# A two-layer DiT block on one core: attention scores laid out with keys on the partitions, row maxima from a separate pass, sums of exponentials on GpSimd

## Chip, cores and metric

One core of a Trainium2 chip. The metric is the device time of one execution in microseconds (us); three runs of the kernel before give a median of 3380.52 us.

## What is computed

Two layers on 2048 tokens of 1024 features and 256 context tokens. The even layer modulates its input, multiplies it by `w_in`, and cuts the product into queries, keys, values and gates of two kinds of heads. It runs softmax attention over context and tokens, multiplies the heads' outputs by silu of the gates, and projects them by `w_out`. The odd layer is a gated MLP with a mixing of tokens in chunks; the change leaves it alone.

```python
def block_attention(q, k, v, scale):          # for blocks of queries
    sc = jnp.einsum('bqhgd,bthd->bhgqt', qi, k).astype(jnp.float32) * scale
    p = jax.nn.softmax(sc, axis=-1).astype(v.dtype)
    return jnp.einsum('bhgqt,bthe->bqhge', p, v)

def even_heads(h, ...):
    cq, ckv, kr, g_a, qb, kb, vb, g_b = jnp.split(h, idx, axis=-1)
    q_a = (rms_norm(cq, a_q_norm) @ a_w_uq).reshape(bsz, n, A_HEADS, A_NOPE + A_ROPE)
    kv_a = (rms_norm(ckv, a_kv_norm) @ a_w_ukv).reshape(bsz, n, A_HEADS, A_NOPE + A_V)
    q_b = rms_norm(qb.reshape(bsz, n, B_HEADS, B_HD), b_q_norm)
    k_b = rms_norm(kb.reshape(bsz, n, B_KV_HEADS, B_HD), b_k_norm)
...
```

There are eight heads of kind A (a latent of low rank; 64 plain and 32 rotary dimensions, values of 64) and eight of kind B (64 dimensions, four query heads to each of two key heads). All rotary parts get an axial rotation. A `rms_norm` divides by the root mean square over features: over 384 latent features for A's queries, over the 64 of a head for B's.

## The kernel before, in words

All products run in a one-pass 32-bit float format (`F32R`) that keeps about 12 significant bits. To keep precision, an operand is split into a high part `h` and a low part `l` (`split`, L57 to L63): ScalarE copies the value into `h`, VectorE subtracts it from the value to give `l`; with `pool=True` GpSimd does both (L59, L60). A product of two split operands is high by high, high by low and low by high.

**Phase 1** computes the product with `w_in` in two halves of the tokens, each in chunks of 512 (`CH`). Activations are feature-major: features on the partitions, tokens along the row. A product (`gemm`) is 24 matmuls of 512 columns into one of the PSUM buffers `ps`; what follows from it is put in `queue` and issued behind the next product (`flush`). B's queries (the loop over `j` in `range(4)`, two chunks each, so eight products per half) are squared on ScalarE, copied with the gain, rotated by `rope` (shuffle L212, products with the tables on GpSimd L213 and VectorE L214, sum L215), split and stored to `QB` by `put`. Their square sums go by `join` and a selection matrix `sel` into one PSUM tile `ssq`; A's query latents (`C3`) are split unnormalised and multiplied by `uq`, and `query_norms` makes one factor 1/rms per query and head from all these sums (`e.rq`). Keys are normalised at once: `rnorm` (L240 to L247) gets the sum on every row from a matmul with ones, takes the root on ScalarE and the RECIPROCAL on VectorE (L246). Between the products run the gates' products and, at a rate per weight tile, the sums for modulation rows needed later (`later_rows`, L267, L276).

**Attention** runs over 16 heads by four groups of 512 queries: 64 groups, the heads of A first, each over 18 tiles of 128 keys (2304 keys). For each of the four tiles of 128 queries of a group, `score` makes the scores with queries on the partitions, in three thirds of 768 keys: three products (A) or two (B, where the 64 dimensions of both parts are stacked on 128 partitions), each as 512 and 256 columns (L605). VectorE scales a third by `e.rq` into SBUF and takes its running maximum (L608); L611 joins the three maxima. `expo` takes exponentials on ScalarE in place (L617), with the sum of each third in `e.parts`. `turn` brings them to keys on partitions: four fp32 transposes of 128x128 on TensorE per key tile (L624), a split of the transposed 128x512 (L62 on ScalarE, L63 on VectorE; every ninth tile on GpSimd by a copy `pf`). `mul` adds V by `ph` and V by `pl` to the output in PSUM (L643), V's high and low parts side by side in 128 columns. At a group's last tile the two halves are added (L647, L648), multiplied by the gate on GpSimd (L649) and stored. `recip` makes 1/sums from `e.parts` in the last four groups, and phase 3 multiplies by them.

The order of the work in attention is written out by hand: each call is a unit with a place in the stream of key tiles, and `units` is sorted by it (L666 and behind). Scores run a group and six tiles ahead, `mul` runs `LAG` = 3 tiles behind `turn`, and the first five tiles of a group some more (`LATE`), since the output's PSUM bank must come free.

**Phase 3** (the output projection and the odd layer) follows; `ring` lays out its first activations in the buffers of keys, values and queries while the last heads run.

Tile pools give each tag a ring of `bufs` buffers; a new tile waits until its buffer's last reader is done.

## Time and profile before

| | us |
|---|---|
| median of three runs (3379.19 to 3383.6) | 3380.52 |
| span of the profiled execution | 3370.8 |
| TensorE busy (17594 instructions) | 3275.9 |
| VectorE busy (4070) | 2472.9 |
| ScalarE busy (3648) | 2000.3 |
| GpSimd busy (603) | 730.2 |

The profile gives for the profiled execution its span, from the first to the last instruction, and no time apart from it; the times of the runs come from outside the program and lie some 10 us higher. Busy times overlap between engines. A matmul's listed duration contains its pipeline, so two that follow each other overlap in the timeline: the distance of their starts, the step, is what the stream costs. The granted clock is the one that the throttle gave TensorE, as a share of full speed.

### The profile page before, as it was taken

What the parts mean: (1) busy time and instruction counts of PE and PEld (TensorE: products, weight loads), DVE (VectorE), ACT (ScalarE), POOL (GpSimd) and SP (SyncE); (2) the same over time, 40 slices, a digit from 0 to 9 for tenths busy, and PEclk for the clock granted to TensorE, in tenths of its full rate; (3) what the DMA queues carried; (4) which work ended last, traced back from release to release, by engine and by line L of the source; (5) the groups of instructions that cost most, each with busy time, mean ns of one, the idle gap of its engine ahead of it and who ended that gap; (6) DMA issues with size and microseconds to landing.
All of it is one profiled execution on the core that took longest, in us unless ns stands there. A gap on an engine that the chain in (4) does not pass through costs nothing.

```text
span 3370.8 us, 47622 instructions
## 1 busy us (share of the span) xinstructions
PE 3275.9 (97%) x17594; PEld 2754.0 (82%) x17594; DVE 2472.9 (73%) x4070; ACT 2000.3 (59%) x3648; POOL 730.2 (22%) x603
## 2 busy tenths in 40 slices
PE   7999999999999999999999999999999899999998
PEld 3787667888888888888888888888778788788787
DVE  4647663488888888888989999999665665765846
ACT  3333332377777777778888888887444253353342
POOL 3413332111111111111222122223222302301201
PEclk9999999999999999999999999999999999999999
DMA  6466654612211221122100010002633343433332
GB/s 230 129 202 207 192 178 142 199 30 55 55 45 39 59 59 42 38 66 61 27 20 23 23 41 23 20 23 49 203 95 113 108 142 113 128 122 113 105 95 75
DMA packets 149083, 311.01 MB, mean 92 GB/s; under 512 B 17762, under 2 KB 43682, under 8 KB 145522
## 3 DMA queue, kind: packets, MB, share of 16 engines
q1 hardware_dynamic: 141058, 280.56, 27.7%
q0 software_dynamic: 7712, 27.28, 2.6%
q8 instruction: 138, 2.26, 0.3%
q14 instruction: 95, 0.78, 0.1%
q10 hardware_dynamic: 80, 0.13, 0.0%
HBM read 237.45 MB, written 70.47 MB: 91 GB/s over the span
## 4 chain that ended last, share of the span: by engine, by line
PE 81%; DVE 6%; issue 4%; DMA 3%; ACT 2%; POOL 1%; SPq 0%; POOLq 0%; ACTq 0%; DVEq 0%
PE s L605 20%; PE o L643 16%; PE pt L624 15%; PE acc L866 3%; PE acc L867 3%; PE acc L868 3%; PE acc L769 3%; PE acc L770 3%; PE acc L771 3%; PE ps L176 3%; PE ps L177 3%; PE ps L178 3%; DMA w<-in_o_w_in 1%; DMA wr<-in_o_w_mod 1%; DMA xr<-in_xT 1%
## 5 line engine op out<-in xcount | busy, mean ns | idle before, releaser
L608 DVE TENSOR_SCALAR_CACHE_REDUCE pr<-s,rq 128x768 f32<-128x768 f32 x768 | 776.0, 1011 | 144.7 <-PE s L605 123.6
L605 PE MATMUL s<-k,q 96*128 96x512 f32 (+3 forms) x3840 | 801.5, 339 | 0.1
L63 DVE TENSOR_TENSOR pl<-pt,ph 128x512 fp32r<-128x512 f32 x1032 | 700.8, 687 | 129.7 <-ACT ph L62 109.1
L62 ACT ACTIVATE ph<-pt 128x512 fp32r<-128x512 f32 x1032 | 605.4, 594 | 267.3 <-PE pt L624 256.6
L617 ACT ACTIVATE pr<-pr,mx 128x768 f32<-128x768 f32 x768 | 715.5, 932 | 58.0 <-DVE mx L611 57.7
L605 PEld LDWEIGHTS s<-k,q 96*128 96x128 f32 (+1 forms) x3840 | 635.5, 188 | 110.3 <-DVE pr L608 1.5
L624 PE MATMUL pt<-ident,pr 128*128 128x128 f32 x4608 | 682.0, 272 | 5.0 <-DVE pl L63 4.8
L624 PEld LDWEIGHTS pt<-ident,pr 128*128 128x128 f32 x4608 | 554.3, 140 | 84.7 <-DVE pl L63 5.8
L643 PE MATMUL o<-ph,v 128*128 128x512 f32 x1152 | 539.3, 468 | 0.3 <-DVE ob L648 0.3
L643 PE MATMUL o<-pl,v 128*128 128x512 f32 x1152 | 453.3, 393 | 0.0
L62 ACT ACTIVATE wh<-w 128x1024 fp32r<-128x1024 f32 x154 | 163.2, 1059 | 466.7 <-PE acc L771 221.4
L63 DVE TENSOR_TENSOR wl<-w,wh 128x1024 fp32r<-128x1024 f32 x154 | 203.5, 1321 | 252.7 <-ACT wh L62 252.6
L59 POOL TENSOR_SCALAR ph<-pf 128x512 fp32r<-128x512 f32 x120 | 74.1, 618 | 1123.0 <-ACT pf L629 1039.8
L176 PE MATMUL ps<-xh,wh 128*128 128x512 f32 (+1 forms) x640 | 249.6, 390 | 6.8 <-POOL xh L167 3.4
L177 PE MATMUL ps<-xl,wh 128*128 128x512 f32 (+1 forms) x640 | 250.2, 391 | 5.3 <-DVE xl L168 5.3
L178 PE MATMUL ps<-xh,wl 128*128 128x512 f32 (+1 forms) x640 | 249.0, 389 | 1.0 <-DVE wl L148 1.0
L643 PEld LDWEIGHTS o<-pl,v 128*128 128x128 f32 x1152 | 221.0, 192 | 5.9 <-DVE pl L63 0.2
L643 PEld LDWEIGHTS o<-ph,v 128*128 128x128 f32 x1152 | 218.7, 190 | 6.3 <-DVE ob L648 0.6
L769 PE MATMUL acc<-wh,k 128*128 128x512 f32 x384 | 155.8, 406 | 28.9 <-DVE y L903 22.6
L60 POOL TENSOR_TENSOR pl<-pf,ph 128x512 fp32r<-128x512 f32 x120 | 154.8, 1290 | 10.0
L770 PE MATMUL acc<-wl,k 128*128 128x512 f32 x384 | 154.4, 402 | 0.5 <-DVE wl L63 0.5
L771 PE MATMUL acc<-wh,k 128*128 128x512 f32 x384 | 153.1, 399 | 0.0
(283 smaller groups left out, 4897.0 us busy)
## 6 DMA issues: line engine op xcount, KB each, us to landing
w<-in_wug SPq DMA_DIRECT2D x64, 512.0 KB, 3.5
wr<-in_w SPq DMA_DIRECT2D x38, 512.0 KB, 4.5
w<-in_e_w_out SPq DMA_DIRECT2D x32, 512.0 KB, 3.5
w<-in_o_w_in SPq DMA_DIRECT2D x32, 512.0 KB, 4.2
w<-in_o_w_out SPq DMA_DIRECT2D x32, 512.0 KB, 3.5
wr<-in_e_w_mod SPq DMA_DIRECT2D x24, 512.0 KB, 6.3
wr<-in_o_w_mod SPq DMA_DIRECT2D x24, 512.0 KB, 4.0
VA<-va SPq DMA_DIRECT2D x18, 512.0 KB, 4.6
```

Of the source, the lines that this page charges most:

```text
L62: e.nc.scalar.activation(h, src, AF.Copy)
L63: e.nc.vector.tensor_tensor(out=l, in0=src, in1=h.bitcast(F32), op=ALU.subtract)
L176: nc.tensor.matmul(out, lhsT=wh(k), rhs=xh(k), start=i == 0, stop=False)
L177: nc.tensor.matmul(out, lhsT=wh(k), rhs=xl(k), start=False, stop=False)
L178: nc.tensor.matmul(out, lhsT=wl(k), rhs=xh(k), start=False, stop=i == n - 1)
L605: nc.tensor.matmul(ps[:, n0:n0 + w], lhsT=a, rhs=b[:, c * SC + n0:c * SC + n0 + w], start=u == 0, stop=u == len(prods) - 1)
L608: nc.vector.tensor_scalar(out=prs[n][:, c * SC:(c + 1) * SC], in0=ps[:, :SC], scalar1=e.rq[:, 4 * g + j, r:r + 1], scalar2=None, op0=ALU.m ...
L617: nc.scalar.activation(x, x, AF.Exp, bias=stats[n][:, 3:4], accum_out=e.parts[:, 4 * g + j, h, c:c + 1])
L624: nc.tensor.transpose(pt[:, j * P:(j + 1) * P], prs[4 * i + j][:, t * P:(t + 1) * P], e.ident)
L643: nc.tensor.matmul(acc[i], lhsT=kv[h][1][:, t, :], rhs=p, start=t + u == 0, stop=t + u == NTT)
L769: nc.tensor.matmul(ps[t], lhsT=h[:, ts], rhs=w[0][:, k, :], start=first, stop=False)
L770: nc.tensor.matmul(ps[t], lhsT=h[:, ts], rhs=w[1][:, k, :], start=False, stop=False)
```

## The change

In phase 1, B's queries are normalised at once like the keys: for each product, `rnorm` (now L241 for its RECIPROCAL, with the softmax scale folded into the root) and a multiply (L346) before `put`. A's latents are normalised before their split (`finish` behind L443, four times three tiles), so `sel`, `ssq`, `join`, `query_norms` and `e.rq` go.

In attention, `score` puts keys on the partitions: one tile of 128 keys by 512 queries, three (A) or two (B) products (L646). The negative maximum of each query is an extra row of the queries against a row of ones in the keys, so that the scores leave PSUM already reduced by it. Exponentials are taken twice from PSUM: into `ph`, rounded to the high part (L655), and in place (L656); VectorE subtracts for `pl` (L657). On tile 8 (A) or tiles 4, 9 and 14 (B), GpSimd splits a copy. `peak` computes the maxima one group ahead, from high parts alone, with queries on the partitions: eight times two matmuls of 512 into a PSUM tile `m` of two banks with one buffer and a reduction of 1024 columns (L611, L613), then four matmuls of 256 and one reduction (L617, L619), and L621 joins them; `row` transposes the four columns of maxima (L629) and ScalarE writes them into the queries' extra row (L631). The sums of exponentials are added tile by tile on GpSimd from `ph` (L663), 14 adds per group of A, 10 of B, 5 in the last four groups; the remaining tiles and the total are summed on TensorE by the matrix `last` (L680, L682), and the low parts by a column of ones behind V. `mul` adds V by `ph` into `oh` (L677) and V's high part by `pl` into `ol` (L678). Queries are loaded two groups ahead.

```diff
+                    def finish(c=c, j=j, o=halves(sq), t=t):
+                        r = rnorm(o, bones, CH, HD, SB)
+                        nc.vector.tensor_tensor(out=t, in0=t, in1=r, op=ALU.mult)
+                        put(t, e.QB[:, j * P:(j + 1) * P, c * CH:(c + 1) * CH])
...
+                        def finish(c=c, o=halves(sqs[c])):
+                            r = rnorm(o, ones, CH, QR, SA)
+                            for i in range(3):
+                                t = ts[c, i]
+                                nc.vector.tensor_tensor(out=t, in0=t, in1=r, op=ALU.mult)
+                                C3[c, i] = unit()
+                                split(e, *C3[c, i], t)
...
+        def peak(i, m):
...
+            pm = pp.tile([P, 2 * CH], F32, name="m", tag="m", bufs=1)
+            if m < 8:
+                j, half = divmod(m, 2)
+                for u in range(2):
+                    k0 = half * 2 * CH + u * CH
+                    nc.tensor.matmul(pm[:, u * CH:(u + 1) * CH], lhsT=Q[:r, 0, j * P:(j + 1) * P], rhs=K[:r, 0, k0:k0 + CH],
+                                     start=True, stop=True)
+                nc.vector.tensor_reduce(out=stats[i][:, j, half:half + 1], in_=pm, axis=AX.X, op=ALU.max)
...
+            ps = pp.tile([P, CH], F32, name="s", tag="s", bufs=4)
...
+                prods = [(K[:m + 1, 0, ks], Q[:m + 1, 0, :]), (K[:m, 1, ks], Q[:m, 0, :]), (K[:m, 0, ks], Q[:m, 1, :])]
...
+                prods = [(K[:, 0, ks], Q[:, 0, :]), (K[:HD + 1, 1, ks], Q[:HD + 1, 1, :])]
...
+            ph = sp.tile([P, CH], F32R, name="ph", tag="ph", bufs=LAG + 4)
+            pl = sp.tile([P, CH], F32R, name="pl", tag="pl", bufs=LAG + 4)
...
+                nc.scalar.activation(ph, ps, AF.Exp)
+                nc.scalar.activation(ps, ps, AF.Exp)
+                nc.vector.tensor_tensor(out=pl, in0=ps, in1=ph.bitcast(F32), op=ALU.subtract)
...
+                nc.gpsimd.tensor_tensor(out=a, in0=tot[i].bitcast(F32), in1=ph.bitcast(F32), op=ALU.add)
...
+            nc.tensor.matmul(oh, lhsT=V[:, t, :2 * DV], rhs=ph, start=first, stop=end)
+            nc.tensor.matmul(ol[:DV + 1], lhsT=V[:, t, DV:2 * DV + 1], rhs=pl, start=first, stop=False)
+            if t not in shares(i)[1]:
+                nc.tensor.matmul(ol[:DV + 1], lhsT=last[:, :DV + 1], rhs=ph, start=False, stop=False)
+            if end:
+                nc.tensor.matmul(ol[:DV + 1], lhsT=last[:, :DV + 1].bitcast(F32), rhs=tot.pop(i), start=False, stop=True)
...
+            for m in range(9):
+                units.append((p0 + 1.6 * m, 1, peak, i, m))
+            units.append((p0 + 1.6 * 8 + 1.9, 1, row, i))
```

TensorE in an A group, mid-stream, before (`pt` is the transposed tile, `pr` the exponentials, `o` the output):

```order
L624 MATMUL pt<-ident,pr 128x128 x4
L643 MATMUL o<-ph,v 128x512
L643 MATMUL o<-pl,v 128x512
L605 MATMUL s<-k,q 128x512
L605 MATMUL s<-k,q 128x256
L605 MATMUL s<-k,q 128x512
L605 MATMUL s<-k,q 128x256
L605 MATMUL s<-k,q 128x512
L605 MATMUL s<-k,q 128x256
L624 MATMUL pt<-ident,pr 128x128 x4
```

and in the change, at the end of the maxima's pass (`m` the scores for the maxima, `nm` the negative maxima):

```order
L611 MATMUL m<-k,q 128x512 x2
L646 MATMUL s<-q,k 128x512 x3
L677 MATMUL oh<-ph,v 128x512
L678 MATMUL ol<-pl,v 65x512
L646 MATMUL s<-q,k 128x512 x3
L677 MATMUL oh<-ph,v 128x512
L678 MATMUL ol<-pl,v 65x512
L617 MATMUL m<-k,q 128x256 x4
```

The transposes are gone, scores are 512 columns wide, and the maxima's matmuls stand between the key tiles.

VectorE around the end of a group, before (`L648` is the add of the output's halves):

```order
L648 TENSOR_TENSOR ob<-o,ob 64x512
L608 TENSOR_SCALAR pr,mx<-s,rq 128x768
L63 TENSOR_TENSOR pl<-pt,ph 128x512 x2
L608 TENSOR_SCALAR pr,mx<-s,rq 128x768
L63 TENSOR_TENSOR pl<-pt,ph 128x512
```

and in the change:

```order
L613 TENSOR_REDUCE mx<-m 128x1
L657 TENSOR_TENSOR pl<-s,ph 128x512
L689 TENSOR_TENSOR ob<-oh,ob 64x512
L691 TENSOR_TENSOR ob<-ol,ob 64x512
L657 TENSOR_TENSOR pl<-s,ph 128x512
L613 TENSOR_REDUCE mx<-m 128x1
```

The scalings of 768 have gone, reductions of 1024 have come, and the output takes two adds.

VectorE in phase 1, B's queries of the second half, before (`L267` is a modulation row's sum):

```order
L212 STREAM_SHUFFLE sq<-t 128x512
L214 TENSOR_TENSOR sq<-sq,ts 128x512
L267 SCALAR_TENSOR_TENSOR acc<-wr,sc,acc 128x512
L215 TENSOR_TENSOR t<-t,sq 128x512
L267 SCALAR_TENSOR_TENSOR acc<-wr,sc,acc 128x512
L63 TENSOR_TENSOR oo<-t,oo 128x512
L148 TENSOR_TENSOR wl<-wr,wh 128x1024
```

and in the change (the lines of the rotation are now L211 to L214, of the sum L262, of the split L65):

```order
L241 RECIPROCAL sq<-sq 128x512
L211 STREAM_SHUFFLE sq<-t 128x512
L346 TENSOR_TENSOR t<-t,sq 128x512
L213 TENSOR_TENSOR sq<-sq,ts 128x512
L262 SCALAR_TENSOR_TENSOR acc<-wr,sc,acc 128x512
L65 TENSOR_TENSOR oo<-t,oo 128x512
L214 TENSOR_TENSOR t<-t,sq 128x512
```

Each product of B's queries gets a RECIPROCAL and a multiply, in front of its split.

## Rows read from the trace of the kernel before

**Rows 1.** The page: busy time by engine; the chain by engine; one of its pieces.

```profile
PE 3275.9 (97%) x17594; PEld 2754.0 (82%) x17594; DVE 2472.9 (73%) x4070; ACT 2000.3 (59%) x3648; POOL 730.2 (22%) x603
...
PE 81%; DVE 6%; issue 4%; DMA 3%; ACT 2%; POOL 1%; SPq 0%; POOLq 0%; ACTq 0%; DVEq 0%
...
88.50 3.35 DVE sq L246
```

**Rows 2.** Windows: stretch, length, busy time by engine, granted clock, DMA share, GB/s.

```profile
92.00:150.00 58.00, 56.79 (x260) 45.01 (x259) 41.74 (x53) 20.23 (x38) 31.23 (x21) 1.00 0.52 151
396.00:465.00 69.00, 59.29 (x247) 44.98 (x248) 65.07 (x79) 19.83 (x36) 34.32 (x22) 0.98 0.70 215
1000.00:1200.00 200.00, 200.00 (x1253) 177.20 (x1251) 162.33 (x312) 151.66 (x300) 35.68 (x35) 1.00 0.16 45
1800.00:1900.00 100.00, 100.00 (x635) 88.30 (x633) 90.79 (x183) 86.78 (x174) 20.40 (x20) 1.00 0.09 23
```

**Rows 3.** Timeline of PE in a group of A: start, duration, instruction.

```profile
1010.13 0.60 PE L624 MATMUL pt<-ident,pr 128*128 128x128 f32 x4
1010.48 0.48 PE L643 MATMUL o<-ph,v 128*128 128x512 f32 x1
1010.80 0.39 PE L643 MATMUL o<-pl,v 128*128 128x512 f32 x1
1011.03 1.21 PE L605 MATMUL s<-k,q 96*128 96x512 f32 x6
1012.07 0.60 PE L624 MATMUL pt<-ident,pr 128*128 128x128 f32 x4
```

**Rows 4.** Timeline of DVE: last add of two groups of A, then of B.

```profile
769.43 0.67 DVE L648 TENSOR_TENSOR ob<-o,ob 64x512 f32<-64x512 f32 x1
...
798.21 0.67 DVE L648 TENSOR_TENSOR ob<-o,ob 64x512 f32<-64x512 f32 x1
...
1598.31 0.68 DVE L648 TENSOR_TENSOR ob<-o,ob 64x512 f32<-64x512 f32 x1
...
1622.96 0.67 DVE L648 TENSOR_TENSOR ob<-o,ob 64x512 f32<-64x512 f32 x1
```

**Rows 5.** Attention's first score (chain) and phase 3's first matmul (timeline).

```profile
660.08 1.06 PE s L605 x6
...
2383.22 0.63 PE L769 MATMUL acc<-wh,k 128*128 128x512 f32 x2
```

**Rows 6.** Timeline of PE in phase 3: first and last of 55 matmuls.

```profile
2500.16 0.39 PE L866 MATMUL acc<-v,wh 128*128 128x512 f32 x1
...
2512.40 0.39 PE L866 MATMUL acc<-q,wh 128*128 128x512 f32 x1
```

**Rows 7.** Timeline of PE in phase 1: fp32 matmuls of 512 columns.

```profile
502.66 2.74 PE L276 MATMUL rows<-acc,pick 128*2 128x512 f32 x6
```

**Rows 8.** Timeline of DVE in a group of A, then in phase 1.

```profile
1019.28 1.01 DVE L608 TENSOR_SCALAR_CACHE_REDUCE pr<-s,rq 128x768 f32<-128x768 f32 x1
1020.21 0.68 DVE L63 TENSOR_TENSOR pl<-pt,ph 128x512 fp32r<-128x512 f32 x1
...
396.72 1.21 DVE L148 TENSOR_TENSOR wl<-wr,wh 128x1024 fp32r<-128x1024 f32 x1
397.86 0.68 DVE L63 TENSOR_TENSOR vt<-pt,vt 128x512 fp32r<-128x512 f32 x1
```

**Rows 9.** Timeline of ACT in attention: three copies from PSUM in a row.

```profile
2363.14 1.56 ACT L62 ACTIVATE ph<-pt 128x512 fp32r<-128x512 f32 x3
```

**Rows 10.** POOL's instructions on two tiles: least, median, most ns; then a group's mean.

```profile
L60 POOL TENSOR_TENSOR pl<-pf,ph x120: 1278/1288/1300, 692.7 to 2284.7; 128x512 fp32r<-128x512 f32 x120
...
L877 POOL TENSOR_TENSOR u<-u,y 128x512 f32<-128x512 f32 x32 | 63.4, 1981 | 404.3 <-ACT y L876 404.3
```

**Rows 11.** DVE in phase 1: reciprocals of the norms; one tile's sums, least, median, most ns.

```profile
L246 DVE RECIPROCAL sq<-sq 128x512 f32<-128x512 f32 x8 | 26.8, 3348 | 5.1 <-ACT sq L245 5.1
...
L215 DVE TENSOR_TENSOR t<-t,sq x32: 662/692/1580, 84.0 to 622.1; 128x512 f32<-128x512 f32 x28, 32x512 f32<-32x512 f32 x4
```

More of the change, by code (lines that the diff above doesn't have):

```diff
@@ L232, in halves, with rnorm @@
             return o
-        def join(out, lhs, o, first=True, last=True):
+        def rnorm(o, lhs, n, width, S=1.0):
+            ss = pp.tile([P, CH], F32, name="ss", tag="misc", bufs=3)
             for i in range(2):
-                nc.tensor.matmul(out, lhsT=lhs, rhs=o[:, i, :], start=first and i == 0, stop=last and i == 1,
-                                 skip_group_check=True)
-        def rnorm(o, lhs, n, width):
-            ss = pp.tile([P, CH], F32, name="ss", tag="misc", bufs=2)
-            join(ss[:, :n], lhs, o)
+                nc.tensor.matmul(ss[:, :n], lhsT=lhs, rhs=o[:, i, :], start=i == 0, stop=i == 1)
             r = tmp(P, n, "sq", 4)
-            nc.scalar.activation(r, ss[:, :n], AF.Sqrt, scale=1.0 / width, bias=e.eps)
+            nc.scalar.activation(r, ss[:, :n], AF.Sqrt, scale=1.0 / (width * S * S), bias=e.epsq[S])
             nc.vector.reciprocal(r, r)
@@ L485, in phase1 @@
                 if half == 1 and i == 1:
-                    e.first = keys(e, 0), queries(e, 0, 0)
+                    e.first = keys(e, 0), [queries(e, 0, g) for g in range(2)]
             assert not aside
@@ new lines, in attention, with shares @@
+        kv, qs, stats, pts = {}, {}, {}, {}
+        acc, tot, gates = {}, {}, {}
+        kv[0], (qs[0], qs[1]) = e.first
+        last = cp.tile([P, DV + 2], F32R, name="last")
+        nc.vector.memset(last[:, :DV].bitcast(F32), 0.0)
+        nc.vector.memset(last[:, DV:].bitcast(F32), 1.0)
+        def shares(i):
+            if i >= NW - NG:
+                return (), (0, 2, 5, 8, 11, 14)
+            if i < NH * NG:
+                return (8,), tuple(t for t in range(16) if t != 8)
+            return (4, 9, 14), tuple(t for t in range(16) if t not in (4, 7, 9, 12, 14))
@@ new lines, in row, with score @@
+        def row(i):
+            h, g = work[i]
+            nm = stats.pop(i)[1]
+            pm = pp.tile([P, 2 * CH], F32, name="m", tag="m", bufs=1)
+            for j in range(4):
+                nc.tensor.transpose(pm[:1, j * P:(j + 1) * P], nm[:, j:j + 1], e.ident)
+            dst = qs[i][NOPE + ROPE:NOPE + ROPE + 1, 0, :] if h < NH else qs[i][HD:HD + 1, 1, :]
+            nc.scalar.activation(dst, pm[:1, :CH], AF.Copy)
+        def score(s):
+            i, t = divmod(s, NTT)
+            h, g = work[i]
+            K, Q = kv[h][0], qs[i]
+            ks = slice(t * P, (t + 1) * P)
+            ps = pp.tile([P, CH], F32, name="s", tag="s", bufs=4)
+            m = NOPE + ROPE
@@ L619, in turn @@
-        def turn(s):
-            i, t = divmod(s, NTT)
-            pt = pp.tile([P, CH], F32, name="pt", tag="pt", bufs=3)
-            for j in range(4):
-                nc.tensor.transpose(pt[:, j * P:(j + 1) * P], prs[4 * i + j][:, t * P:(t + 1) * P], e.ident)
-            ph = sp.tile([P, CH], F32R, name="ph", tag="ph", bufs=LAG + 2)
-            pl = sp.tile([P, CH], F32R, name="pl", tag="pl", bufs=LAG + 2)
-            if t % 9 == 8 and i < len(work) - NG:
+                nc.tensor.matmul(ps, lhsT=a, rhs=b, start=u == 0, stop=u == len(prods) - 1)
@@ L652, in recip @@
-        def recip(b):
-            qs = slice(4 * b, 4 * b + 4)
-            nc.vector.tensor_reduce(out=e.sums[:, qs, :], in_=e.parts[:, qs], axis=AX.X, op=ALU.add)
-            nc.vector.reciprocal(e.sums[:, qs, :], e.sums[:, qs, :])
-            rp = pp.tile([P, CH], F32, name="rp", tag="pt", bufs=3)
-            for j in range(4):
-                nc.tensor.transpose(rp[:2 * NH, j * P:(j + 1) * P], e.sums[:, 4 * b + j, :], e.ident)
-            rs = sp.tile([2 * NH, CH], F32, name="rs", tag="pf", bufs=2)
-            nc.scalar.activation(rs, rp[:2 * NH, :], AF.Copy)
-            cs = slice(b * CH, (b + 1) * CH)
-            nc.sync.dma_start(e.R1[:, cs], rs)
@@ L666, in attention @@
[L666 to L674 removed]
+                acc[i] = [pp.tile([P, CH], F32, name="o" + q, tag="o" + q, bufs=1) for q in "hl"]
@@ L675, in attention @@
+        for s in range(NW * NTT):
+            units.append((s, 2, score, s))
             t = s % NTT
```

238 lines of the change are left out of this document (106 added, 132 removed).

## The prediction, made before the change was timed

> **What bounds the kernel now.** I read the page's busy times and chain first [rows 1]: TensorE (PE) is busy 97% of the 3370.8 us span and makes 81% of the chain. Then the windows [rows 2]: in both kinds of attention heads PE has no gap, at a granted clock of 1.00, while VectorE (DVE) stands at 81% (A) and 91% (B), ScalarE (ACT) at 76% and 87%, GpSimd (POOL) at 18% and 20%. So attention costs what PE streams, and a faster PE would soon meet DVE. Phase 1 is mixed: in 92 to 150 PE has 56.8 of 58 us, but in 396 to 465 only 59.3 of 69, with DVE at 65.1: there DVE paces. The chain's row at 88.50 [rows 1] is a RECIPROCAL of 3.35 us: a norm on DVE can already be exposed.
>
> The PE timeline of an A group [rows 3] gives the steps, start to start: four transposes 0.35 (1010.13 to 1010.48), the two products with V 0.32 and 0.23, a score pair of 512 and 256 columns 0.347 (1.04 for three pairs, 1011.03 to 1012.07). The first product behind the transposes costs some 0.09 more than the second; I call that a switch. A group has 36 pairs and 18 of the rest: 12.5+16.2 = 28.7. From one group's last add to the next's [rows 4] it is 28.78 in A and 24.66 in B, so the steps explain the period. Attention lasts from the first score, 660.08, to phase 3's first matmul, 2383.22 [rows 5]: 1723 us.
>
> **PE in attention.** Dense matmuls of 512 columns step by 0.227 (2500.16 to 2512.40 is 54 steps) [rows 6]. A group of A now has 54 score products, 16 maxima, 36 products with V and three sums by `last`: 109 x 0.227 = 24.7. The four maxima of 256 columns cost 0.347-0.227 each, 0.48 together. The four transposes of the maxima I put at 0.58 (0.35, two switches, rounded up). The final sum in plain fp32 runs as two instructions, like the modulation rows' sums, of 2.74/6 = 0.46 each [rows 7], 0.91, and two switches, 1.1. Together 26.9 against 28.78. B: 36+16+36+7 = 95 matmuls, 21.6, and the same 2.2: 23.7 against 24.66. So PE saves only 1.9 and 0.9 us a group: the transposes were cheap, and the maxima take most of it back.
>
> **What covers the rest of attention.** DVE: a scaling of 768 steps 0.93 (1019.28 to 1020.21), an op of 1024 steps 1.14 (396.72 to 397.86) [rows 8]. A reduction of 1024 from PSUM is not in the trace. Its bounds: 1.14, and the scaling's duration 1.01 x 1024/768 = 1.35. I take 1.15, since the row of the same width is the nearest. A subtraction of 512 steps 0.61 (0.68 less the overlap of 0.07 that the 1024 row shows). A: 9 x 1.15 + 17 x 0.61 + two adds 1.2 + 0.15 = 22.1 of 27; B, with 15 subtractions, 20.9 of 24. All reductions lie in 13 of a group's 18 key tiles; there DVE has 18.2 of PE's 20.7 us in A, 17.6 of 18.4 in B: covered, but tight in B. ACT: three ops of 512 take 1.56 [rows 9], so A's 35 exponentials 18.2, and with copies under 20.5. A tile holds one of the four `s` buffers some 4.3 us (scores 0.68, two exponentials 1.1, subtraction 0.68, a reduction in its way 1.15, hand-overs 0.7); four tiles of PE last 5.3 to 6.
>
> POOL: A has 14 adds x 1.29 (the 128x512 subtraction there, 1278 to 1300 ns) [rows 10] + 1.9 for the parts + 1.3 for the gate = 21.3; B 10 x 1.29 + 5.7 + 1.3 = 19.9. The other row of such an add, L877 in phase 3, has a mean of 1.98: the upper bound. I take 1.29, being from attention. PE's final sum waits for the last add, tile 15's, which has five tiles or 7 us. The gate product stands behind adds, and SP's store of O waits for it; what is queued behind on SP, the queries two groups ahead, has a whole group to spare. That, and the sums' way through DRAM before phase 3, I cost at nothing; without the cover attention would get the DMA share that the chain has as a whole, 3% [rows 1], 0.03 x 1723 = 52 us.
>
> With small stalls I take 27.0 and 24.0. The prologue is new: nine maxima run before the first score, and with one `m` buffer PE and DVE alternate, 9 x (0.45+1.15+0.25) and the row: 17 to 18. Nothing fills PE meanwhile; should it run slower after the gaps, some 5 more: I take 23. Attention: 23 + 32 x 27.0 + 28 x 24.0 + the last four groups with 12 sums on PE, 3 x 25 + 21 (the last has no next maxima) + 4 to drain = 1659, **-64**.
>
> **Phase 1.** The query norms move here. DVE gets 20 RECIPROCALs of 3.35 [rows 11] (16 for the QB products, four before uq), 67 us, and 28 multiplies at 0.69 (L215 on the same operands, up to 1.58 beside POOL), 19: 86 us in all. PE shows of it what DVE cannot fit. Half 0: 41.7 + 8 x 4.04 = 74.0 in 58 us, 16.0 too much; the ring of four `sq` tiles, three of them per product, lets PE lead by about two products of 24 x 0.227, 10.9: 5 exposed. Half 1: 65.1+32.3-69 = 28.4, less 10.9: 17.5. Before uq, reciprocal, multiply and split (3.35+0.69+0.68, and 1.4 for each further part) follow the square sums, with one gate product of 5.4 as cover: 5 per half, 10. The joins and small transposes that go give back 3. **+30** (bounds: +5, if idle DVE time takes all but part of the uq waits; +86, nothing hidden). POOL gets memsets of ones, SP one more query group to load, both early: nothing.
>
> Phase 3 differs by the shape of two rings and keeps PE's work: nothing.
>
> **Sum.** 3370.8-64+30 = 3337 of span. The page has no time of the profiled execution apart from its span; the median of the three runs, 3380.5 (3379.2 to 3383.6), lies 9.7 us above it, and I keep that: **3346 us**. Some 0.2% (7 us) is what a measurement can tell from no change.
>
> **Rivals.**
> Better on both counts: periods 26.9 and 23.7, prologue 17 (1644), phase 1 at +5: 3380.5-79+5 = 3307. For it: PE had no gap before with DVE at 91%. Against: DVE already paces part of phase 1. Chance 0.22.
>
> Phase 1 hides nothing, the other side: each RECIPROCAL and multiply shows in full, +86 in place of +30: 3402. From 64+7 = 71 exposed it is slower. For it: the 88.50 row and 10 us of idle PE in 396 to 465. Against: DVE had 16 us free in 92 to 150. 0.13.
>
> POOL as bound: adds at 1.98 make A 14 x 1.98+3.2 = 30.9 and B 26.8, 3.9 and 2.8 more a group: +203, 3549. At 1.69 (A) they do nothing yet. Against: 120 subtractions in attention took 1.28 to 1.30. The Trainium skill (GPSIMD Engine Reference, 8. Key points) says that GpSimd shares its SBUF interfaces with VectorE, suffers beside VectorE instructions with two SBUF inputs, and is about half as fast elementwise, which speaks against moving sums there. By that rule the adds would keep 1.29, as DVE's subtractions read PSUM; the 1278 to 1300 rows agree. 0.07.
>
> DVE as bound: a reduction at 1.35 gives B's stretch 19.4 for PE's 18.4, 1.0 for 28 groups, and waits at the one `m` buffer, 0.4 for 60: +52, 3398. The Trainium skill (VectorE: DVE Perf Modes, Rules for kernel authors) calls tensor_reduce the slowest DVE operation and advises restructuring; no row here shows one this wide. 0.13.
>
> A late hand-over that I cost at nothing (query loads, the row of maxima, the keys' ones): up to the 52 us above, 3346 to 3398. 0.08.
>
> **Numbers.** My forecast has 0.37, its own range is 3325 to 3368. **3295 to 3405** takes in the better case and most of the phase 1, DVE and late cases, and leaves out the POOL case and the tails. Faster by over 0.2% (below 3374): 0.22+0.37, and 0.05 of the slow cases at part of their price: 0.64. Within 0.2%: 0.11 of them. Slower: 0.25.
>
> **What would show it.** Right: last adds 27 us apart in A and 24 in B, PE over 98% busy there, DVE near 85%, POOL 80% with adds of 1.29; the stretches of the QB products longer by 5 and 17 us, PE waiting for results of the normalising multiplies; phase 3's first matmul near 2349. Wrong: reductions over 1.3, PE waiting on `s` or `m`, adds near 2 us, phase 1 longer by over 60.

## The result and the profile after

The changed kernel takes 3534.26 us (median of four runs, 3531.93 to 3536.28) against 3379.86 (four runs, 3378.41 to 3383.6): 1.0458 times the time before, 95% interval 1.0443 to 1.0473. It is 154 us slower; forecast were 34 us faster, and the range ended at 3405. By stages of the profiled executions:

| stage, us | before | forecast | after | after - forecast |
|---|---|---|---|---|
| phase 1, to attention's first matmul | 660.1 | 690.1 | 709.5 | +19.4 |
| first maxima to first score | none | 23 | 23.3 | +0.3 |
| from there to the 32nd group's last add (A) | | 864 | 883.5 | +19.5 |
| 28 groups of B | 690.7 | 672 | 784.2 | +112.2 |
| last four groups | | 96 | 115.1 | +19.1 |
| last add to phase 3's first matmul | | 4 | 9.9 | +5.9 |
| phase 3 | 987.6 | 987.6 | 1004.7 | +17.1 |
| outside the span | 9.7 | 9.7 | 4.2 | -5.5 |

The last column adds up to 188, from 3346 to 3534. The last row is not time outside the program, as it was taken to be: each timed run on record lies only some 1.8 us above its own span (3531.93 and 3530.1 for the profiled execution of the change). So the 9.7 is mostly that the profiled execution of the kernel before was some 8 us faster than its median, and a few us of any difference between before and after in the table can be that.

The page after (busy times by engine; the chain by engine), against [rows 1]:

```profile
PE 3302.6 (94%) x13998; PEld 2463.1 (70%) x13998; DVE 2526.6 (72%) x3022; ACT 1903.6 (54%) x3287; POOL 1690.5 (48%) x1369
...
PE 76%; issue 6%; DVE 6%; POOL 6%; ACT 3%; DMA 1%; POOLq 0%; SPq 0%; ACTq 0%; DVEq 0%
```

POOL is on the chain with 6%. The same windows as [rows 2], and a long one in B (columns as there):

```profile
92.00:150.00 58.00, 51.62 (x227) 39.86 (x227) 56.17 (x50) 17.95 (x32) 26.58 (x17) 1.00 0.32 100
396.00:465.00 69.00, 56.42 (x226) 42.84 (x224) 62.96 (x61) 21.32 (x35) 25.92 (x18) 0.92 0.52 155
1000.00:1200.00 200.00, 200.00 (x874) 148.79 (x873) 167.67 (x213) 152.48 (x280) 157.40 (x128) 1.00 0.22 54
1800.00:1900.00 100.00, 89.63 (x366) 60.01 (x364) 74.89 (x97) 68.02 (x128) 66.92 (x60) 0.98 0.10 27
...
1700.00:2300.00 600.00, 543.31 (x2221) 368.32 (x2222) 448.37 (x571) 405.31 (x762) 413.77 (x362) 0.98 0.10 27
```

A is dense on PE, as forecast. In B, from 1700 to 2300, no engine is: PE 91%, DVE 75%, ACT 68%, POOL 69%. That is the picture of a wait, not of a full engine. The last adds of two groups of A and two of B (DVE's timeline; before: [rows 4]), and PE's waits from 1700 to 2300 (total us, times, longest):

```profile
821.79 0.68 DVE L691 TENSOR_TENSOR ob<-ol,ob 64x512 f32<-64x512 f32 x1
849.12 0.68 DVE L691 TENSOR_TENSOR ob<-ol,ob 64x512 f32<-64x512 f32 x1
...
1805.54 0.68 DVE L691 TENSOR_TENSOR ob<-ol,ob 64x512 f32<-64x512 f32 x1 [1.08 <-ACT su L690]
1833.66 0.68 DVE L691 TENSOR_TENSOR ob<-ol,ob 64x512 f32<-64x512 f32 x1 [1.07 <-ACT su L690]
```

```profile
PE ol L678 <- POOL pl L62: 46.8, 42, 2.0
PE oh L677 <- ACT ph L655: 9.0, 21, 0.4
```

Periods, from last add to last add: on average 27.33 in A (27.0 forecast, 28.78 before) and 28.36 in B (24.0 forecast, 24.66 before). PE waits twice per group of B for a low part from GpSimd, once some 2 us and once some 0.2. POOL's and PE's timelines of one group show it:

```profile
1834.42 1.27 POOL L692 TENSOR_TENSOR ob<-ob,gt 64x512 f32<-64x512 f32 x1 [6.34 <-DVE ob L691]
1835.65 1.28 POOL L663 TENSOR_TENSOR sa<-ph 128x512 f32<-128x512 f32 x1
1837.01 2.67 POOL L663 TENSOR_TENSOR sa<-sa,ph 128x512 f32<-128x512 f32 x2
1839.65 0.61 POOL L61 TENSOR_SCALAR ph<-pf 128x512 fp32r<-128x512 f32 x1
1840.24 1.27 POOL L663 TENSOR_TENSOR sa<-sa,ph 128x512 f32<-128x512 f32 x1
1841.47 1.26 POOL L62 TENSOR_TENSOR pl<-pf,ph 128x512 fp32r<-128x512 f32 x1
...
1840.32 0.50 PE L677 MATMUL oh<-ph,v 128*128 128x512 f32 x1
1842.78 0.44 PE L678 MATMUL ol<-pl,v 128*65 128x512 f32 x1 [1.96 <-POOL pl L62]
...
1844.37 0.63 PE L677 MATMUL oh<-ph,v 128*128 128x512 f32 x1
```

GpSimd stands idle for 6.3 us behind the gate product at the head of its queue, then has three adds, half a split, a fourth add and the other half to do, while the group's first scores come in a burst; tile 4's low part ends at 1842.7. After the wait the granted clock is 0.5 (1.2 in place of 2.4 GHz) from 1844.0 to 1847.4: PE's matmuls there take 0.63 and step 0.43. This comes once in three or four groups (0.98 in the window's mean).

### The profile page after: what moved, and what is told of

It is laid out like the page before. It is cut to its first block, busy times and chain, and to the rows that moved or that the text cites. A ratio compares the mean times of both kernels' runs of the same rounds, so it can differ in the third digit from the quotient of the medians.

```text
span 3530.1 us, 40728 instructions
## 1 busy us (share of the span) xinstructions
PE 3302.6 (94%) x13998; PEld 2463.1 (70%) x13998; DVE 2526.6 (72%) x3022; ACT 1903.6 (54%) x3287; POOL 1690.5 (48%) x1369
## 4 chain that ended last, share of the span: by engine, by line
PE 76%; issue 6%; DVE 6%; POOL 6%; ACT 3%; DMA 1%; POOLq 0%; SPq 0%; ACTq 0%; DVEq 0%
PE s L646 18%; PE ol L678 7%; PE oh L677 7%; PE m L611 6%; PE acc L816 4%; PE acc L815 4%; PE acc L817 4%; PE acc L913 3%; PE acc L912 3%; PE acc L914 3%; PE ps L176 3%; PE ps L177 3%; PE ps L175 3%; PE ol L680 2%; POOL pl L62 2%
## 5 line engine op out<-in xcount | busy, mean ns | idle before, releaser
L663 POOL TENSOR_TENSOR sa<-sa,ph 128x512 f32<-128x512 f32 x684 | 881.4, 1289 | 181.7 <-ACT ph L655 151.9
L646 PE MATMUL s<-q,k 96*128 96x512 f32 (+3 forms) x2880 | 924.1, 409 | 1.0 <-ACT q L631 0.7
L655 ACT ACTIVATE ph<-s 128x512 fp32r<-128x512 f32 x1036 | 620.2, 599 | 391.3 <-PE s L646 348.1
L657 DVE TENSOR_TENSOR pl<-s,ph 128x512 fp32r<-128x512 f32 x1036 | 693.3, 684 | 122.6 <-ACT s L656 108.1
L613 DVE TENSOR_REDUCE mx<-m 128x1 f32<-128x1024 f32 x512 | 624.0, 1219 | 208.4 <-PE m L611 207.4
L646 PEld LDWEIGHTS s<-q,k 96*128 96x128 f32 (+3 forms) x2880 | 545.8, 191 | 194.8 <-issue 22.2
L656 ACT ACTIVATE s<-s 128x512 f32<-128x512 f32 x1036 | 617.5, 596 | 0.0
L678 PE MATMUL ol<-pl,v 128*65 128x512 f32 x1152 | 458.6, 400 | 67.3 <-POOL pl L62 56.3
L677 PE MATMUL oh<-ph,v 128*128 128x512 f32 x1152 | 466.0, 407 | 13.3 <-ACT ph L655 11.8
L64 ACT ACTIVATE wh<-w 128x1024 fp32r<-128x1024 f32 x154 | 163.2, 1059 | 488.1 <-PE acc L817 220.2
L65 DVE TENSOR_TENSOR wl<-w,wh 128x1024 fp32r<-128x1024 f32 x154 | 219.7, 1427 | 270.8 <-ACT wh L64 254.9
L611 PE MATMUL m<-k,q 96*128 96x512 f32 (+1 forms) x1024 | 330.0, 404 | 9.7 <-DVE mx L613 9.7
L677 PEld LDWEIGHTS oh<-ph,v 128*128 128x128 f32 x1152 | 218.9, 190 | 105.0 <-ACT ph L655 40.8
L678 PEld LDWEIGHTS ol<-pl,v 128*65 128x65 f32 x1152 | 159.6, 139 | 138.3 <-POOL pl L62 76.9
L611 PEld LDWEIGHTS m<-k,q 96*128 96x128 f32 (+1 forms) x1024 | 185.5, 191 | 80.1 <-DVE mx L613 33.0
L815 PE MATMUL acc<-wh,k 128*128 128x512 f32 x384 | 158.0, 412 | 31.2 <-DVE y L949 19.1
```

The source lines that it names most:

```text
L611: nc.tensor.matmul(pm[:, u * CH:(u + 1) * CH], lhsT=Q[:r, 0, j * P:(j + 1) * P], rhs=K[:r, 0, k0:k0 + CH], start=True, stop=True)
L613: nc.vector.tensor_reduce(out=stats[i][:, j, half:half + 1], in_=pm, axis=AX.X, op=ALU.max)
L646: nc.tensor.matmul(ps, lhsT=a, rhs=b, start=u == 0, stop=u == len(prods) - 1)
L655: nc.scalar.activation(ph, ps, AF.Exp)
L656: nc.scalar.activation(ps, ps, AF.Exp)
L657: nc.vector.tensor_tensor(out=pl, in0=ps, in1=ph.bitcast(F32), op=ALU.subtract)
```

## Experiments

Single runs, but four of the kernel with half the keys; the kernel before lay between 3374.6 and 3383.5 in the seven runs beside the last of them, so a few us are noise. Periods are means over 26 groups of B or 30 of A; in the five runs whose edits leave B alone B's period lies at 28.32 to 28.40, so a tenth of a us in a period is more than noise. Each edit is against the changed kernel unless said otherwise.

### Group B: what holds it

**GpSimd's queue.** First the gate product:

```diff
-                (nc.vector if i >= NW - NG else nc.gpsimd).tensor_tensor(out=ob[:DV], in0=ob[:DV], in1=gates.pop(i)[:DV], op=ALU.mult)
...
+            with tc.issue_after(marks[i + 1]) if i + 1 in marks else ExitStack():
+                eng.tensor_tensor(out=ob[:DV], in0=ob[:DV], in1=gates.pop(i)[:DV], op=ALU.mult)
```

> Only edit: GpSimd's product with the gate (L692) is queued behind the low part of the next group's first tile that GpSimd splits (tile 4 in B, tile 8 in A) instead of ahead of the next group's adds. Theory Q (the gate product stands first in GpSimd's queue and waits up to 6.3 us for the end of the output, so the next group's adds and tile 4's split start late, and PE waits for that tile's low part): in B the wait of PE's L678 for L62, 51 us from 1700 to 2380, falls below 10, the B period goes from 28.2 us to 25.5 to 26, and the time from 3534 to 3460 to 3480. Rival L (GpSimd carries too much in B, whatever the order): the wait stays or moves to tile 9, the time stays within 15 us of 3534. A stays at 27.4 under both.

3508.79; B 27.83. PE's wait hardly falls:

```profile
PE ol L680 <- POOL pl L62: 42.4, 43, 1.8
```

Theory Q falls for the most part: with the gate product out of the way GpSimd waits for the first exponentials instead (166.7 us from 1700 to 2300, 7.0 at most), and is as late with tile 4. Rival L's 15 us are passed too (25). Then no split at all in B, and two splits further on:

```diff
-            return (4, 9, 14), tuple(t for t in range(16) if t not in (4, 7, 9, 12, 14))
+            return (), tuple(t for t in range(16) if t not in (4, 7, 9, 12, 14))
```

> Only edit: in B no tile is split on GpSimd; ScalarE takes both exponentials and VectorE the subtraction of tiles 4, 9 and 14 too (3 x 0.61 us more per group on VectorE, 3 x 1.9 less on GpSimd). Theory Q and rival L both: PE no longer waits for L62, B goes to 24.5 to 25.5 us, the time to 3435 to 3465. Rival V (VectorE with nine reductions of 1.22 and the group's end bound B, GpSimd's wait only follows): VectorE at some 23 us of work per group keeps B at 27 or more, the time above 3505.

3469.25; B 26.09. The wait is gone and 2.27 us per group with it, though VectorE has three subtractions more; the 24.5 to 25.5 expected are not reached. With `(8, 13)` in that place:

> Only edit: in B two tiles, 8 and 13, are split on GpSimd in place of 4, 9 and 14; adds as before plus none. Theory B (the first tiles of a group are scored in a burst while the output's PSUM banks come free, GpSimd then has three adds, a split and another add between its two halves to do at once, and tile 4's low part is late; tiles further on are not): no wait for L62 over 0.5 us, B at 25 to 26 us, better than or equal to the 26.1 of no split at all, the time 3440 to 3470. Rival (a split on GpSimd is late wherever it stands in B, since adds come ahead of it): the wait stays with tiles 8 and 13, B over 27, the time over 3495.

3496.26; B 27.02, the wait falls to a third (16.7 us from 1700 to 2300, 0.7 at most) and doesn't go. The numbers are the rival's: tile 4 is a worse place, but these splits too cost more than they save (26.09 without any). They cost it not by GpSimd's lateness alone: PE now also waits 13.5 us, 22 times, for the row of maxima from ScalarE.

**What remains.** Maxima 1.8 tiles apart (`p0 + 1.8 * m`, the row at 15.9 instead of 14.7), no splits in B:

> No split on GpSimd in B, and the nine maxima passes of each group set 1.8 tiles apart in place of 1.6 (the last at tile 14.7 in place of 13.1, the row of maxima 1.2 tiles later). Theory E (of the 26.1 us of B without splits, 2 to 3 are because PE outruns ScalarE's two exponentials of 1.0 to 1.1 us per tile where no maxima stand between, and is held by them and VectorE where they do): B at 25 to 25.6, A at 27.0 or 27.3, the time 3440 to 3455 against 3469. Rival (the waits are those of the group's end, where the row, the copies of the output and the burst of scores meet): no gain, or a loss since the row comes closer to the first score that needs it.

3459.4; B 25.14, A 27.59. Theory E is borne out in B; A loses 0.26, so from here on only B is spread. Then fewer sums on PE:

```diff
-            return (), tuple(t for t in range(16) if t not in (4, 7, 9, 12, 14))
+            return (), tuple(range(15))
```

> In B no splits on GpSimd, maxima passes 1.8 tiles apart in B alone, and 15 of 18 tiles of exponentials summed on GpSimd in place of 11, so 3 sums by the matrix on PE in place of 7. Theory P (with the splits gone PE is the bound in B, GpSimd has room: 14 x 1.29 + 1.3 = 19.4 of 24): B from 25.14 to 24.2 to 24.6, A back at 27.3, the time 3420 to 3440. Rival (VectorE and ScalarE bound B by now, at 22.9 and 21.6 us of work in bursts): B stays within 0.3 us of 25.14, the time at 3450.

3468.94; B 25.75: four matmuls less, 0.6 us more. PE's work isn't the bound there; why it became slower, which neither theory had, stays open. Then the load of VectorE, of ScalarE, and the lag, each on the base of B without splits and with spread maxima (in B alone, B 25.13 by a later run on the same B):

```diff
-                nc.vector.tensor_reduce(out=stats[i][:, j, half:half + 1], in_=pm, axis=AX.X, op=ALU.max)
+                nc.vector.tensor_reduce(out=stats[i][:, j, half:half + 1], in_=pm if h < NH else pm[:, :CH], axis=AX.X, op=ALU.max)
...
-            nc.scalar.activation(dst, pm[:1, :CH], AF.Copy)
+            nc.scalar.activation(dst, pm[:1, :CH], AF.Copy, scale=1.0 if h < NH else 1.25)
```

> B without splits and with its maxima 1.8 tiles apart (B 25.14 in the spread run); in B the eight reductions read 512 of the 1024 columns, so the maxima are those of part of the keys, and the row is taken 1.25 times to keep the exponentials finite (the output loses accuracy, the work of PE and ScalarE is the same). VectorE has 8 x 0.5 = 4 us less per B group. Theory V (VectorE, with 22.5 us of work in 25, sets B): B at 23.9 to 24.3. Rival A (ScalarE's two exponentials do): B stays within 0.4 of 25.1. A at 27.3 under both; the time 3470 at 25.1, some 3440 at 24.0.

```diff
-                nc.scalar.activation(ps, ps, AF.Exp)
+                if h < NH:
+                    nc.scalar.activation(ps, ps, AF.Exp)
```

> The same base; in B the second exponential, in place in PSUM, is left out, so the low part is not the exponentials' and B's outputs are not the reference's. ScalarE has 18 x 0.5 = 9 us less per B group, the buffer of scores comes free 0.5 us earlier. Rival A (ScalarE sets B): B at 23.5 to 24.2. Theory V: B stays at 24.7 to 25.2.

```diff
-    LAG = 3
+    LAG = 4
```

> The same base, and the products with V run four tiles behind the scores in place of three in all groups (one buffer more of each part, all orders shift with it). Theory H (no engine is full; PE waits 0.3 to 0.5 us at each of some four tiles of a group because the way score, two exponentials, subtraction, with a reduction in between, is longer than three tiles where no maxima pass stands): those waits go, B at 24.2 to 24.6, A at 26.6 to 27.0, the time 3435 to 3455. Theory V or A (throughput of one engine): both within 0.3 of before, the time 3465 to 3475.

Half the reductions: B 23.90 (3409.53), as theory V had it. Half the exponentials: 26.37 (3481.22), which neither had. Four tiles of lag: 25.26 (3450.55), within 0.3 of 25.14, so the lag isn't it. The window 1750 to 2200, all in B: the change, then without splits, spread, and spread with half reductions:

```profile
1750.00:2200.00 450.00, 408.46 (x1668) 276.96 (x1669) 337.32 (x430) 303.99 (x571) 311.11 (x272) 0.98 0.10 28
```

```profile
1750.00:2200.00 450.00, 437.78 (x1811) 296.03 (x1811) 393.39 (x518) 353.40 (x673) 244.10 (x191) 1.00 0.11 30
```

```profile
1750.00:2200.00 450.00, 445.33 (x1880) 309.14 (x1879) 407.02 (x537) 365.96 (x697) 251.51 (x197) 1.00 0.11 31
```

```profile
1750.00:2200.00 450.00, 450.00 (x1977) 330.20 (x1976) 362.12 (x566) 391.99 (x735) 266.78 (x208) 1.00 0.12 33
```

The run goes with theory V: with 4 us less on VectorE per group, PE is dense and B is at PE's own work, 23.7 by the forecast's count. Before that VectorE was busy 90% (407.02 of 450), the fullest of the engines beside PE. Two reserves. The scheduler places PE's instructions anew with these edits, so the 1.24 us are load and order together. And a shorter reduction also gives the one buffer `m` back sooner (0.68 us for 1.22): in the spread run VectorE is not full, it waits 52.2 us from 1700 to 2300 for the maxima's matmuls, and in 36 of 161 passes from 1750 to 2200 the next of these starts within 0.15 us of the end of a reduction. No run gave `m` a second buffer, so VectorE's load and this hand-over aren't told apart. A reader of the second line should also see that PE "busy" 97% was not PE full: the same 450 us hold 1811 instructions there and 1977 at the end. A matmul is drawn 0.39 us long at a step of 0.23, so a wait of up to 0.16 us leaves no gap. That relieving ScalarE made B slower (26.37) is not explained; there PE waits 0.7 us once per group for a low part from VectorE, and the order of scores and products with V is another from the first group on. It speaks against rival A, no more.

So of 28.36-23.90 = 4.46 us, taken away in this order: 2.27 the splits on GpSimd, 0.95 the spacing of the maxima, 1.24 the longer reductions.

### The end of attention

```diff
-                (nc.vector if i >= NW - NG else nc.gpsimd).tensor_tensor(out=ob[:DV], ...)
+                nc.gpsimd.tensor_tensor(out=ob[:DV], ...)
```

> Only edit: the product with the gate of the last four groups stands on GpSimd, as in all other groups, instead of VectorE. Theory K (VectorE's product of two SBUF operands at 2460.49 took 12.08 us, against 0.68 elsewhere, because GpSimd's queue had no gap from 2444 to 2472; PE then waited 10.7 us for a low part): no VectorE instruction there over 1.3 us, PE's wait of 10.7 gone, the last four groups some 10 us shorter, the time near 3524. Rival: the wait was for something else (a load of the gate); then it shows on GpSimd and holds the store of the last outputs, the time stays at 3534 or grows.

3523.28, 11 us less; the last four groups take 105.9 us for 115.1, and no wait of PE over 3.3 us is left in them. What it removed, in the change (DVE, POOL, PE):

```profile
2460.49 12.08 DVE L692 TENSOR_TENSOR ob<-ob,gt 64x512 f32<-64x512 f32 x1
...
2471.39 0.64 POOL L61 TENSOR_SCALAR q<-zt 128x512 fp32r<-128x512 f32 x1
2472.11 1.58 POOL L62 TENSOR_TENSOR q<-zt,q 128x512 fp32r<-128x512 f32 x1
...
2473.22 0.69 PE L678 MATMUL ol<-pl,v 128*65 128x512 f32 x1 [10.74 <-DVE pl L657]
```

VectorE's product of two SBUF operands, 0.67 to 0.68 us in the three other groups, ends at 2472.6, just behind the first gap (2472.03 to 2472.11) in GpSimd's stream, which is back to back from 2447.4. The Trainium skill (GPSIMD Engine Reference, 8. Key points) says that GpSimd shares its SBUF interfaces with VectorE and contends with VectorE instructions that have two SBUF inputs; the 12.08 against 0.68 agrees.

The last sums' way to DRAM and back was then moved off SP's queue as well:

```diff
-            nc.sync.dma_start(rs, view(e.SU))
+            q = nc.scalar if b == NG - 1 else nc.sync
+            q.dma_start(rs, view(e.SU))
...
-            nc.sync.dma_start(view(e.R1), rs)
+            q.dma_start(view(e.R1), rs)
```

> Two edits at attention's end: the gate products of the last four groups on GpSimd (as in the tail run), and the last block's reading of the sums, and the store of their reciprocals, issued from ScalarE's queue in place of SP's. Theory W (phase 3's first weights are issued from SP's queue at 2519.86 only, behind that store, which waits for the sums' way out to DRAM, back and through the reciprocal; PE then waits 10.5 us for their split): the weights are issued ahead of the last group's end, PE's first wait of phase 3 falls below 2 us, the time is 8 to 11 us under the 3523 of the gate products alone: 3512 to 3515. Rival (the weights wait for SBUF that attention's last tiles hold): the wait stays, the time 3520 or more.

3521.93. The weights go out 4.7 us earlier than with the gate products alone (2504.29 for 2509.01), but PE's wait of 10.3 there for the high part becomes 6.0 for the high and 4.7 for the low part, since GpSimd's splits now wait 3.58 us for the store of O and 2.95 for that of the reciprocals. The time doesn't move, as the rival had it, but not by the rival's cause as far as SP's timeline shows:

```profile
2503.98 0.22 SPq L693 DMA_DIRECT2D SU<-su  x1
2504.29 0.93 SPq L790 DMA_DIRECT2D w<-in_e_w_out  x2
```

The weights follow directly on another store in SP's queue, that of the last group's sums (L693), which waits for the group's end. So the edit didn't take the weights out of that line, and theory W was only half tested; before, they went out at 2370.98, 12.2 us ahead of PE's first use.

### Phase 1

```diff
-            nc.scalar.activation(r, ss[:, :n], AF.Sqrt, scale=1.0 / (width * S * S), bias=e.epsq[S])
-            nc.vector.reciprocal(r, r)
+            nc.scalar.activation(r, ss[:, :n], AF.Ln, scale=1.0 / (width * S * S), bias=e.epsq[S])
+            nc.scalar.activation(r, r, AF.Exp, scale=-0.5)
```

> Only edit: 1/rms comes from two ScalarE functions, exp(-0.5 ln(x)), instead of a root on ScalarE and a RECIPROCAL of 3.35 us on VectorE; all 28 norms, the keys' too. Theory R (VectorE's RECIPROCALs pace phase 1; the chain product by product is 9.3 to 10 us in the QB products against PE's 5.9): QB's products come 6 to 7 us apart, the first pass for maxima starts 35 to 50 us earlier than 709.5, the time is 3485 to 3500. Rival S (ScalarE's way, GpSimd's halves or the multiplies with two SBUF operands pace it, and ScalarE's table loads, 116 in place of 60, come on top): it starts less than 15 us earlier, or later.

The first maxima start at 707.4 for 709.5 (3528.7). Against the expectation of theory R, taking VectorE's RECIPROCALs away gains 2 us. The timeline of one product of the change (DVE, ACT, POOL, PE; other work of these engines left out) shows a ring:

```profile
457.15 3.34 DVE L241 RECIPROCAL sq<-sq 128x512 f32<-128x512 f32 x1
461.05 0.67 DVE L346 TENSOR_TENSOR t<-t,sq 128x512 f32<-128x512 f32 x1
461.75 0.63 ACT L64 ACTIVATE oo<-t 128x512 fp32r<-128x512 f32 x1 [5.07 <-DVE t L346]
462.29 0.61 ACT L229 ACTIVATE oq<-sq 128x512 fp32r<-128x512 f32 x1
464.28 1.43 POOL L230 TENSOR_TENSOR oq<-sq,oq 128x512 fp32r<-128x512 f32 x1
465.76 0.80 PE L238 MATMUL ss<-oq,bones 128*128 128x512 f32 x1 [2.07 <-POOL oq L230]
466.60 0.69 ACT L240 ACTIVATE sq<-ss,eps 128x512 f32<-128x512 f32 x1 [3.69 <-PE ss L238]
467.84 3.34 DVE L241 RECIPROCAL sq<-sq 128x512 f32<-128x512 f32 x1
```

ScalarE's copy L64 waits for the multiply, and L229, the next product's squares, stands behind it in the queue; POOL, PE and ScalarE follow in turn, and the next RECIPROCAL starts 10.7 us later. VectorE is not idle meanwhile: with the rotations, the splits and the modulation rows' sums it is busy 102.57 of the 105 us from 435 to 540, so its load alone could set this pace. With ln and exp it is busy 69.48 of 105 and the stores of the products still come mostly 8.6 to 9.1 us apart: ScalarE's longer part, two table loads of 1.28 us among it, takes RECIPROCAL's place in the ring. So the store was moved one product back:

```diff
                         r = rnorm(o, bones, CH, HD, SB)
-                        nc.vector.tensor_tensor(out=t, in0=t, in1=r, op=ALU.mult)
-                        put(t, e.QB[:, j * P:(j + 1) * P, c * CH:(c + 1) * CH])
+
+                        def store():
+                            nc.vector.tensor_tensor(out=t, in0=t, in1=r, op=ALU.mult)
+                            put(t, e.QB[:, j * P:(j + 1) * P, c * CH:(c + 1) * CH])
+
+                        queue.append(store)
```

> Only edit: in phase 1 the multiply, split and store of one of B's query products come one product later (behind the next but one product's matmuls), the norm itself where it was. Theory O (a loop through the engines' in-order queues, not VectorE's load, paces these products: ScalarE's copy of the split waits for RECIPROCAL and multiply, and the copy of the next product's squares stands behind it, which the next norm's sum on PE needs; about 10 us a turn): the copy of the squares no longer waits for a RECIPROCAL of the product before, the products come at VectorE's own 8.5 to 9 us apart, phase 1 is 10 to 20 us shorter, the time 3515 to 3525. Theory R (VectorE's load alone): no change within 6 us.

> The later multiply, split and store of the run before, and the norms by exp(-0.5 ln(x)) on ScalarE without RECIPROCAL. Theory O: either edit alone leaves the other limit (the loop, or VectorE's load), both together take both away: products 6 to 7 us apart, the first pass for maxima at 672 to 685 in place of 709.5, the time 3495 to 3510. Rival (ScalarE's table loads or the products with two SBUF operands beside GpSimd pace it): within 10 us of the run with the later store alone.

First maxima at 708.8 (3532.55) with the later store alone, as theory R had it, and at 684.5 (3506.18) with both, as theory O. The window 435 to 540 in the change, with ln and exp, with the later store, and with both (columns as in [rows 2]; VectorE's busy time is the third):

```profile
435.00:540.00 105.00, 87.56 (x336) 67.25 (x337) 102.57 (x95) 37.81 (x61) 35.94 (x24) 0.90 0.48 142
435.00:540.00 105.00, 88.70 (x346) 69.04 (x344) 69.48 (x80) 65.65 (x88) 38.54 (x26) 0.92 0.42 142
435.00:540.00 105.00, 85.83 (x344) 67.68 (x345) 100.10 (x96) 38.61 (x62) 36.73 (x25) 0.90 0.44 146
435.00:540.00 105.00, 98.55 (x396) 75.78 (x397) 64.17 (x78) 63.31 (x87) 33.67 (x25) 0.96 0.50 162
```

Alone the later store meets VectorE's load, ln and exp alone meet the ring; together 25 of the 49 us that phase 1 had grown by are back. What the other 24 are was not tried. Part of them is the clock: in phase 1 the granted clock is 0.5 for 65 us of the change and for 48 us with both edits, against 27 us before; at half speed that is at most 19 and 10 us more than before.

### Whether a version of the change wins

Put together in one kernel (B without splits, spread, 15 tiles on GpSimd, whose loss was not known yet; the end; phase 1), and then A's split off GpSimd too:

> All edits so far that helped in one kernel: B without splits, its maxima 1.8 tiles apart, 15 tiles summed on GpSimd; the gate products of the last groups on GpSimd, the last reciprocals by ScalarE's queue; in phase 1 the later multiply and store and norms by ln and exp. If the parts add (theory: they are separate places), 3534 less 70 to 100 in B, 20 at the end, 28 in phase 1: 3385 to 3415, level with or slower than the kernel before (3380). If the kernel before is beaten, below 3374.

> The run before with A's one split (tile 8) off GpSimd too, and 16 tiles summed there. Theory E (ScalarE and VectorE in bursts): A has PE work of 26.0 and 27.3 measured; VectorE takes 0.61 more: A 27.0 to 27.5, the time within 10 us of the run before. Theory B (any split on GpSimd delays PE): A falls to 26.3 to 26.8, the time 15 to 30 us under it.

3441.26, above the 3385 to 3415 expected (28 times 0.6 of it by the 15 tiles), and 3429.37; A's median period is 27.27 for 27.37, as theory E had it, and 7.5 of the 12 us come after the last group. With 11 tiles of B on GpSimd again, and then, from that, a maximum over half of B's keys (`for u in range(2 if h < NH else 1)` and the shorter reduction), and a longer lag with one split:

> The run with A's split off GpSimd too, but with 11 tiles of B summed on GpSimd and 7 on PE as in the change (B 25.75 with 15 and 3). Expected by the earlier runs: B 25.1, all else as there: 3429 - 28 x 0.6 = 3412. Slower than the kernel before (3378) if the prologue, phase 1's remaining 24 us, B's and the last groups' excess are as they were.

> The last kernel (3413), and in B the maxima come from half of the keys: one matmul of 512 and one reduction of 512 in place of two matmuls and 1024, and the row is taken 1.25 times. The softmax does not depend on the value that is subtracted, but the guard against overflow is now one for these inputs, not for all. VectorE loses 8 x 0.5 = 4 us per B group, PE 8 x 0.227 = 1.8. Theory V (VectorE binds B, PE next): B from 25.13 to 22.0 to 22.6, the time 3413 - 28 x 2.8 = 3335, 3325 to 3345, under the kernel before (3380). Rival (ScalarE's 20.5 us with its bursts binds next): B at 23 to 24, the time 3355 to 3380.

> The kernel of 3413 with exact maxima, but four tiles of lag and one split of B, tile 9, on GpSimd. Theory V with B (VectorE has 0.61 less; the split's low part has a tile more of time, so PE does not wait for it): B from 25.13 to 24.5 to 24.7, the time near 3400. Rival (a split on GpSimd holds PE even with four tiles): PE waits for L62 again, B over 25.3, the time 3415 to 3440.

3413.16 with exact maxima, for 3412 expected: 1% slower than before, by single runs. With half the keys 3319.23 (3318.03 to 3321.13): 0.9823 times the kernel before, interval 0.9807 to 0.984, B 22.08 with PE dense. This beats both kernels on these inputs, but the subtracted value is no longer the maximum, so an overflow is no longer ruled out; I don't call it a substitute. The longer lag with one split: 3460.53, B 26.62, which neither expectation had; PE's waits for GpSimd's low parts are only 4.6 us from 1700 to 2300, and why it costs 1.5 us a group stays open.

## Why the prediction was wrong

**Right:** PE's own work. A's 26.9 with 27.0 forecast is 27.33; B's 23.7 is met as soon as nothing holds PE (23.90, half reductions). The prologue's 23 is 23.3, at a granted clock of 0.61 from 709 to 733. GpSimd's adds keep their 1.29 (median 1289 ns), a reduction of 1024 its step of 1.14 (1.22 long). So no price of one instruction was far off. (In the better case the terms add up to 1641, not 1644; nothing hangs on it.)

**Wrong, 112 us:** the step that failed is the cover in B: "B, with 15 subtractions, 20.9 of 24 ... covered, but tight in B", and GpSimd's 19.9 of 24. Both were averages over a group, and what decides is the order in the queues. GpSimd's 69% did not keep tile 4's low part from being late (2.27 us a group, run without splits). In the timeline adds that nobody waits for yet stand ahead of it; no run put the splits ahead of the adds, so that part is read, not tested. The rival "POOL as bound" had the engine and not the mechanism. The maxima in 13 of 18 tiles made the stretch uneven (0.95), and the reductions cost 1.24 more, by VectorE's load (90% busy with the splits back on it), the order of PE's work or the hold of the one buffer `m`. The rival "DVE as bound", with its waits at `m`, came nearest to that, at 0.13 and with a price (1.35 a reduction) that it didn't need. The Trainium skill (VectorE: DVE Perf Modes, Rules for kernel authors) calls tensor_reduce the slowest DVE operation and advises restructuring. The advice would have helped: halving eight reductions per group gives 1.24 us of 25.14. Its reason is not what the trace shows, with 1.22 us for a reduction of 1024 columns and 3.34 for a RECIPROCAL of 512.

**Wrong, 19 us:** phase 1's exposure. Exposed were 14.8 and 20.3 us in the QB products of the two halves and 8.7 and 5.1 before uq (by the distance of the stores of KB and KA, of KR and QN, in the two traces), for 5, 17.5 and 10. The overlap that failed is "the ring of four `sq` tiles, three of them per product, lets PE lead by about two products of 24 x 0.227, 10.9", and most of all in half 0: of the 16.0 us that VectorE can't fit there, 14.8 show, so PE led by next to nothing. PE's sum for each norm waits for a copy on ScalarE that stands behind VectorE's work on the product before; VectorE's load and this ring hold the products to about the same pace (10.7 us in the one shown). In half 1, 20.3 of 28.4 show. The sum had no term for PE's clock in phase 1, at most 19 us here.

**Wrong, 19 + 6 + 17 us:** the end. "That, and the sums' way through DRAM before phase 3, I cost at nothing" is the step that failed, and phase 3 at nothing. PE's wait for phase 3's first weights is 10.5 us where before it has none; they stand in SP's queue behind the last sums. VectorE's product held out for 12 us, 9 of the first 19, was not thought of at all. Of phase 3's 17 us some 7 are lost in the first 120 us, where a wait of 9.5 for the next weights stands against 5.1 before. The other 10 come bit by bit, with PE's listed waits no longer than before (35.6 us for 36.2) and the granted clock at 0.5 for 66 us in place of 43; their cause stays open, and the fast profiled execution of the kernel before may be part of it.

**A's +19.5** is 31 periods of 0.35, with PE without a gap, and 9 us in the first group. There PE is without a gap too, but runs 143 instructions to a group's 119, since the next group's scores and maxima come in, at a granted clock of 0.92; so part of the 9 is work that the last groups are spared.
